# A softmax over 32768 columns: 64 KB per partition in each transfer and three buffers, in place of 32 KB and six

## The chip, the cores and the metric

The kernel runs on one core of a Trainium2 chip. Two of its engines do the arithmetic here: DVE (the vector engine) and ACT (the scalar engine). SP only issues transfers, and 16 DMA engines carry them out. The metric is device time in microseconds (us) of one execution. "Span" is the same execution as the profile sees it; it is about 1.8 us shorter than the device time.

## The reference

```python
def reference(logits, temperature):          # logits (16, 256, 32768) float32, temperature 1.0
    scaled = logits / temperature
    scaled = scaled - scaled.max(axis=-1, keepdims=True)
    exp_scaled = np.exp(scaled)
    return (exp_scaled / exp_scaled.sum(axis=-1, keepdims=True)).astype(np.float32)
```

There are 4096 rows of 128 KB each. All of them must be read once and written once: 536.87 MB in each direction, 1073.74 MB in all.

## The kernel before

A row is cut into four quarters, and 128 quarter rows (32 KB per partition, 4 MB in all) make a tile. There are 128 tiles. Neighbouring partitions hold parts of the same row, so the maximum and the sum are combined over groups of four partitions, in two rounds of shuffle and combine. Each half of a quarter has its own maximum (`nm`) and sum, and a small set of operations turns them into one factor per half (`f`).

```python
_W = 8192; _BUFS = 6; _AHEAD = 4; _CC = 4096; _SCALE_ON_DVE = {1, 4, 7}
...
        for c in range(NCH):                                  # two pieces of 4096 columns
            nc.vector.tensor_reduce(out=nm[:, c:c+1], in_=xc, axis=X, op=A.max, negate=True)
            ...
            nc.scalar.activation(out=xc, in_=xc, func=Exp, bias=nm[:, c:c+1], ..., accum_out=ssum[:, c:c+1])
        ...                                                   # 12 small DVE records more for the combines
        for c in range(NCH):
            if (t * NCH + c) % 8 in _SCALE_ON_DVE:
                nc.vector.tensor_scalar_mul(out=xc, in0=xc, scalar1=f[:, c:c+1])
            else:
                nc.scalar.activation(out=xc, in_=xc, func=Copy, scale=f[:, c:c+1])

    for t in range(min(_AHEAD, n_tiles)):
        load(t)
    for t in range(n_tiles):
        compute(t)
        store(t)
        if t + _AHEAD < n_tiles:
            load(t + _AHEAD)
```

All loads and stores are issued from one queue (SP), in program order: a load that waits for its buffer also holds up the stores that come after it.

Of the kernel before, what the change touches and what calls it, by code (L numbers as in the profile page):

```python
# [1 line left out]

# [4 lines left out]


_W = 8192
_BUFS = 6  # L10
_AHEAD = 4
_CC = 4096
_SCALE_ON_DVE = {1, 4, 7}


@with_exitstack
def kernel(
    ctx: ExitStack,
    tc: tile.TileContext,
    logits: bass.AP,  # L20
    temperature: bass.AP,
    out: bass.AP,
):
    nc = tc.nc
    inv_t = 1.0 / float(temperature)
    P = nc.NUM_PARTITIONS
    fp32 = mybir.dt.float32
    Exp = mybir.ActivationFunctionType.Exp
    Copy = mybir.ActivationFunctionType.Copy
    X = mybir.AxisListType.X  # L30
    A = mybir.AluOpType

    xf = logits.flatten_outer_dims()
    of = out.flatten_outer_dims()
    N, V = xf.shape
    W = min(_W, V)
    SPLIT = V // W
    assert SPLIT * W == V and (N * SPLIT) % P == 0 and W % _CC == 0
    x = xf.rearrange("n (h v) -> (n h) v", h=SPLIT)
    o = of.rearrange("n (h v) -> (n h) v", h=SPLIT)  # L40
    n_tiles = N * SPLIT // P
    n_rounds = SPLIT.bit_length() - 1
    NCH = W // _CC

    xpool = ctx.enter_context(tc.tile_pool(name="x", bufs=_BUFS))
    spool = ctx.enter_context(tc.tile_pool(name="stats", bufs=8))
    slots = {}

    def load(t: int) -> None:
        xs = xpool.tile([P, W], fp32, tag="x", name="xs")  # L50
        slots[t] = xs
        tc.keep_in_program_order(
            nc.sync.dma_start(out=xs, in_=x[t * P : (t + 1) * P, :])
        )

    def store(t: int) -> None:
        tc.keep_in_program_order(
            nc.sync.dma_start(out=o[t * P : (t + 1) * P, :], in_=slots.pop(t))  # L58
        )

    def combine(v, op) -> None:
        for j in range(n_rounds):
            mask = [i ^ (1 << j) for i in range(32)]
            nc.vector.stream_shuffle(  # L64
                out=v[:, j + 1 : j + 2], in_=v[:, j : j + 1], mask=mask
            )
            nc.vector.tensor_tensor(  # L67
                out=v[:, j + 1 : j + 2],
                in0=v[:, j : j + 1],
                in1=v[:, j + 1 : j + 2],  # L70
                op=op,
            )

    def compute(t: int) -> None:
        xs = slots[t]
        nm = spool.tile([P, NCH], fp32, tag="nm", name="nm")
        ssum = spool.tile([P, NCH], fp32, tag="ssum", name="ssum")
        ee = spool.tile([P, NCH], fp32, tag="ee", name="ee")
        f = spool.tile([P, NCH], fp32, tag="f", name="f")
        ttj = spool.tile([P, NCH], fp32, tag="ttj", name="ttj")  # L80
        nMh = spool.tile([P, 1 + n_rounds], fp32, tag="nMh", name="nMh")
        Sh = spool.tile([P, 1 + n_rounds], fp32, tag="Sh", name="Sh")
        rS = spool.tile([P, 1], fp32, tag="rS", name="rS")

        for c in range(NCH):
            xc = xs[:, c * _CC : (c + 1) * _CC]
            nc.vector.tensor_reduce(  # L87
                out=nm[:, c : c + 1], in_=xc, axis=X, op=A.max, negate=True
            )
            if inv_t != 1.0:  # L90
                nc.vector.tensor_scalar_mul(
                    out=nm[:, c : c + 1], in0=nm[:, c : c + 1], scalar1=inv_t
                )
            nc.scalar.activation(  # L94
                out=xc,
                in_=xc,
                func=Exp,
                bias=nm[:, c : c + 1],
                scale=inv_t,
                accum_out=ssum[:, c : c + 1],  # L100
            )

        with tc.high_priority():
            nc.vector.tensor_reduce(out=nMh[:, 0:1], in_=nm, axis=X, op=A.min)  # L104
            combine(nMh, A.min)
            nc.scalar.activation(  # L106
                out=ee,
                in_=nm,
                func=Exp,
                bias=nMh[:, n_rounds : n_rounds + 1],  # L110
                scale=-1.0,
            )
            nc.vector.tensor_tensor_reduce(  # L113
                out=ttj,
                in0=ee,
                in1=ssum,
                scale=1.0,
                scalar=0.0,
                op0=A.mult,
                op1=A.add,  # L120
                accum_out=Sh[:, 0:1],
            )
            combine(Sh, A.add)
            nc.vector.reciprocal(out=rS, in_=Sh[:, n_rounds : n_rounds + 1])  # L124
            nc.scalar.activation(out=f, in_=ee, func=Copy, scale=rS)  # L125

        for c in range(NCH):
            xc = xs[:, c * _CC : (c + 1) * _CC]
            if (t * NCH + c) % 8 in _SCALE_ON_DVE:
                nc.vector.tensor_scalar_mul(out=xc, in0=xc, scalar1=f[:, c : c + 1])  # L130
            else:
                nc.scalar.activation(out=xc, in_=xc, func=Copy, scale=f[:, c : c + 1])  # L132

    for t in range(min(_AHEAD, n_tiles)):
        load(t)
    for t in range(n_tiles):
        compute(t)
        store(t)
        if t + _AHEAD < n_tiles:
            load(t + _AHEAD)  # L140


# [1 line left out]
_INS = ['logits', 'temperature']  # L144
_OUTS = [((16, 256, 32768), 'float32')]

_NUMBERS = {'temperature': 1.0}


# [26 lines left out]
```

## Time and profile before

| | before |
|---|---|
| device time, median of the runs at hand when predicting | 2506.95 us (2502.8 to 2507.95) |
| span of the profiled run | 2500.8 us |
| DVE busy, ACT busy | 63%, 65% |
| DMA, GB/s over the span | 429 |

These are lines of the page of the kernel before: busy time and number of instruction records by engine, then the busy tenths of the DMA engines in 40 slices of the span with the GB/s that they moved, then the packets and the queues (q1 carries the kernel's own transfers, q14 the instructions).

```profile
span 2500.8 us, 4102 instructions
...
DVE 1564.4 (63%) x2400; ACT 1625.0 (65%) x929; POOL 0.2 (0%) x4
...
DMA  9999999999999999999999999999999999999997
GB/s 406 429 432 431 431 434 433 431 434 434 431 436 433 431 435 433 432 434 432 432 436 431 432 435 433 432 435 433 431 435 433 431 435 433 431 435 433 431 434 325
...
q1 hardware_dynamic: 36864, 1073.76, 99.6%
q14 instruction: 32, 0.26, 0.0%
```

DMA is at its limit from the first slice to the last, while both compute engines idle for a third of the time. The Trainium skill, "DMA: Bandwidth & Descriptors", section "Where 436 GB/s comes from", gives a ceiling of 435.2 GB/s; the trace agrees as far as it goes, no window of 600 us being above 435. The same section names about 358 GB/s on the DRAM side as what binds such transfers; this kernel moved 429 over its span, so that figure did not bind here. An estimate from the ceiling: at 435.2 GB/s the bytes need 2467 us, so a change of this kind can win at most some 34 us of the 2500.8.

The windows view splits the span into stretches. The columns are: start and end, length, busy us and instructions of DVE, ACT and POOL, PE clock, DMA share, GB/s.

```profile
400.00:1000.00 600.00, 376.43 (x582) 394.36 (x225) 0.00 (x0) 1.00 1.00 433
1000.00:1600.00 600.00, 377.06 (x581) 391.82 (x225) 0.00 (x0) 1.00 1.00 433
1600.00:2200.00 600.00, 379.09 (x573) 388.73 (x221) 0.00 (x0) 1.00 1.00 433
...
2485.00:2490.00 5.00, 0.00 (x0) 0.00 (x0) 0.00 (x0) 1.00 0.78 334
2490.00:2495.00 5.00, 0.00 (x0) 0.00 (x0) 0.00 (x0) 1.00 0.06 26
2495.00:2501.00 6.00, 0.00 (x0) 0.00 (x0) 0.00 (x0) 1.00 0.04 16
```

A share of 0.06 is one of 16 engines: one DMA engine is still working at its full 26 GB/s when the other 15 are done. A transfer is complete only when all 16 engines have done their part, so the engine that is furthest behind sets the pace of the whole kernel.

### The profile page before, as it was taken

The page shows a single profiled execution, that of the slowest core. Times are in us where ns is not written, and L with a number is a line of the kernel's source. Part 1 is how long each engine was busy: PE and PEld are TensorE (multiplying, and loading weights), DVE is VectorE, ACT ScalarE, POOL GpSimd, SP SyncE. Part 2 cuts the span into 40 slices and gives each one's busy share as a digit, 9 for nine tenths or more (in the row PEclk, how much of TensorE's full clock was granted, in tenths as well). Part 3 has the DMA queues.
Part 4 walks back from the last instruction along what each step waited for, and adds up shares of the span by engine and source line. Part 5 has one row for each costly group of instructions (what it writes and reads, how often), then busy time and mean ns, then how long its engine had stood idle before and what let it go on. Part 6 is the DMA issues. An engine that isn't in the chain of part 4 may idle for free.

```text
span 2500.8 us, 4102 instructions
## 1 busy us (share of the span) xinstructions
DVE 1564.4 (63%) x2400; ACT 1625.0 (65%) x929; POOL 0.2 (0%) x4
## 2 busy tenths in 40 slices
DVE  6666566666566665666666666666666666666564
ACT  6766666666666666666666666666666666666664
POOL 0000000000000000000000000000000000000000
DMA  9999999999999999999999999999999999999997
GB/s 406 429 432 431 431 434 433 431 434 434 431 436 433 431 435 433 432 434 432 432 436 431 432 435 433 432 435 433 431 435 433 431 435 433 431 435 433 431 434 325
DMA packets 36896, 1074.02 MB, mean 429 GB/s; under 512 B 4096, under 2 KB 4096, under 8 KB 4096
## 3 DMA queue, kind: packets, MB, share of 16 engines
q1 hardware_dynamic: 36864, 1073.76, 99.6%
q14 instruction: 32, 0.26, 0.0%
HBM read 536.87 MB, written 536.87 MB: 429 GB/s over the span
## 4 chain that ended last, share of the span: by engine, by line
DMA 76%; DVE 10%; ACT 8%; another core or an unknown queue 4%; issue 0%; SPq 0%; ACTq 0%
DMA xs<-in_logits_dram 47%; DMA out_dram<-xs 29%; DVE nm L87 9%; ACT xs L132 4%; ACT xs L94 4%; DVE Sh L67 0%; DVE Sh L64 0%; ACT f L125 0%; ACT ee L106 0%; DVE rS L124 0%; DVE ttj L113 0%; SPq L58 0%; DVE xs L130 0%; DVE nMh L67 0%
## 5 line engine op out<-in xcount | busy, mean ns | idle before, releaser
L87 DVE TENSOR_REDUCE nm<-xs 128x1 f32<-128x4096 f32 x256 | 1119.6, 4414 | 432.9 <-DMA xs<-in_logits_dram 432.9
L94 ACT ACTIVATE xs<-xs,nm 128x4096 f32<-128x4096 f32 x256 | 949.1, 3707 | 677.5 <-DVE nm L87 677.5
L132 ACT ACTIVATE xs<-xs,f 128x4096 f32<-128x4096 f32 x160 | 589.9, 3705 | 4.1
L113 DVE CUSTOM_DVE_ANT_0 ttj<-ee,ssum 128x2 f32<-128x2 f32 x128 | 20.5, 160 | 391.5 <-ACT ee L106 382.9
L130 DVE TENSOR_SCALAR xs<-xs,f 128x4096 f32<-128x4096 f32 x96 | 225.9, 2353 | 41.0 <-ACT f L125 39.7
L125 ACT ACTIVATE f<-ee,rS 128x2 f32<-128x2 f32 x128 | 37.8, 295 | 159.0 <-DVE rS L124 159.0
L94 ACT ACTIVATION_READ_ACCUMULATOR xs<-xs,nm 128x1 f32 x256 | 47.7, 187 | 0.0
L67 DVE TENSOR_TENSOR nMh<-nMh 128x1 f32<-128x1 f32 x256 | 40.8, 159 | 8.6
L67 DVE TENSOR_TENSOR Sh<-Sh 128x1 f32<-128x1 f32 x256 | 40.8, 159 | 8.6
L64 DVE STREAM_SHUFFLE nMh<-nMh 128x1 f32<-128x1 f32 x256 | 38.8, 151 | 0.0
L64 DVE STREAM_SHUFFLE Sh<-Sh 128x1 f32<-128x1 f32 x256 | 38.7, 151 | 0.0
L106 ACT ACTIVATE ee<-nm,nMh 128x2 f32<-128x2 f32 x128 | 35.8, 280 | 0.0
L124 DVE RECIPROCAL rS<-Sh 128x1 f32<-128x1 f32 x128 | 21.0, 164 | 4.3
L104 DVE TENSOR_REDUCE nMh<-nm 128x1 f32<-128x2 f32 x128 | 19.8, 155 | 4.3
L113 DVE DVE_READ_ACCUMULATOR2_ANT Sh<- 128x1 f32 x128 | 10.6, 83 | 0.0
L64 DVE LOAD_MASK_SELECT Sh<-Sh x256 | 3.6, 14 | 10.8
L64 DVE LOAD_MASK_SELECT nMh<-nMh x256 | 3.6, 14 | 10.8
L94 ACT ACT_TABLE_LOAD x1 | 1.3, 1283 | 13.1 <-DMA xs<-in_logits_dram 13.1
L157 POOL MEMSET const-bfloat16-1.0<- 128x1 bf16 x1 | 0.1, 101 | 0.0
L157 POOL MEMSET const-uint8-127<- 128x1 uint8 x1 | 0.1, 101 | 0.0
L157 POOL MEMSET const-float32-0.0<- 128x1 f32 x1 | 0.1, 98 | 0.2 <-issue 0.2
L157 POOL MEMSET const-float32-1.0<- 128x1 f32 x1 | 0.1, 98 | 0.0
## 6 DMA issues: line engine op xcount, KB each, us to landing
xs<-in_logits_dram SPq DMA_DIRECT2D x128, 4096.0 KB, 48.4
out_dram<-xs SPq DMA_DIRECT2D x128, 4096.0 KB, 49.6
```

Of the source, the lines that this page charges most:

```text
L64: nc.vector.stream_shuffle(out=v[:, j + 1 : j + 2], in_=v[:, j : j + 1], mask=mask)
L67: nc.vector.tensor_tensor(out=v[:, j + 1 : j + 2], in0=v[:, j : j + 1], in1=v[:, j + 1 : j + 2], op=op,)
L87: nc.vector.tensor_reduce(out=nm[:, c : c + 1], in_=xc, axis=X, op=A.max, negate=True)
L94: nc.scalar.activation(out=xc, in_=xc, func=Exp, bias=nm[:, c : c + 1], scale=inv_t, accum_out=ssum[:, c : c + 1],)
L104: nc.vector.tensor_reduce(out=nMh[:, 0:1], in_=nm, axis=X, op=A.min)
L106: nc.scalar.activation(out=ee, in_=nm, func=Exp, bias=nMh[:, n_rounds : n_rounds + 1], scale=-1.0,)
L113: nc.vector.tensor_tensor_reduce(out=ttj, in0=ee, in1=ssum, scale=1.0, scalar=0.0, op0=A.mult, op1=A.add, accum_out=Sh[:, 0:1],)
L124: nc.vector.reciprocal(out=rS, in_=Sh[:, n_rounds : n_rounds + 1])
L125: nc.scalar.activation(out=f, in_=ee, func=Copy, scale=rS)
L130: nc.vector.tensor_scalar_mul(out=xc, in0=xc, scalar1=f[:, c : c + 1])
L132: nc.scalar.activation(out=xc, in_=xc, func=Copy, scale=f[:, c : c + 1])
L157: nc = _bacc.Bacc("TRN2", target_bir_lowering=False, num_devices=1)
```

## The change

The intent is fewer and larger packets, half as many small operations, and a shorter start and end. A tile becomes 128 half rows (64 KB per partition, 8 MB), of which three fit. The loads of the first and last tiles and the last store are moved in pieces of 16 KB per partition. A tile has four pieces of 4096 columns, each scaled by DVE (2560 columns) and ACT (1536 columns) together. The multiplication that makes the factors moves from ACT to DVE. Only one round of combining is left.

```diff
-_W = 8192
-_BUFS = 6
-_AHEAD = 4
-_CC = 4096
-_SCALE_ON_DVE = {1, 4, 7}
+_SPLIT = 2
+_CW = 16384
+_BUFS = 3
+_PIECE = 4096
+_LAST_DMA = 4096
+_DVE_SHARE = 0.625
 ...
+    def load(i: int) -> None:
+        g, c = divmod(i, C)
+        xs = xpool.tile([P, CW], fp32, tag="x", name="xs")
+        slots[i] = xs
+        for s, n in spans(CW, _LAST_DMA if g in (0, G - 1) else CW):
+            ... nc.sync.dma_start(out=xs[:, s : s + n], in_=x[...])
 ...
-            nc.scalar.activation(out=f, in_=ee, func=Copy, scale=rS)
+            nc.vector.tensor_scalar_mul(out=f, in0=ee, scalar1=rS)
 ...
+            cut = int(n * _DVE_SHARE) // 512 * 512
+            nc.vector.tensor_scalar_mul(
+                out=xs[:, s : s + cut], in0=xs[:, s : s + cut], scalar1=f[:, k : k + 1]
+            )
+            nc.scalar.activation(
+                out=xs[:, s + cut : s + n], in_=xs[:, s + cut : s + n],
+                func=Copy, scale=f[:, k : k + 1],
+            )
 ...
+    order = [("L", i) for i in range(min(_BUFS, n_chunks))] + [("S", 0)]
+    for i in range(1, n_chunks):
+        order.append(("S", i))
+        if i + _BUFS - 1 < n_chunks:
+            order.append(("L", i + _BUFS - 1))
```

More of the change, by code (lines that the diff above doesn't have):

```diff
@@ L35, with spans, piece, store @@
     N, V = xf.shape
-    W = min(_W, V)
-    SPLIT = V // W
-    assert SPLIT * W == V and (N * SPLIT) % P == 0 and W % _CC == 0
-    x = xf.rearrange("n (h v) -> (n h) v", h=SPLIT)
-    o = of.rearrange("n (h v) -> (n h) v", h=SPLIT)
-    n_tiles = N * SPLIT // P
-    n_rounds = SPLIT.bit_length() - 1
-    NCH = W // _CC
+    W = V // _SPLIT
+    CW = min(_CW, W)
+    C = W // CW
+    assert W * _SPLIT == V and CW * C == W and (N * _SPLIT) % P == 0
+    x = xf.rearrange("n (h v) -> (n h) v", h=_SPLIT)
+    o = of.rearrange("n (h v) -> (n h) v", h=_SPLIT)
+    G = N * _SPLIT // P
+    n_chunks = G * C
+    n_rounds = _SPLIT.bit_length() - 1
     xpool = ctx.enter_context(tc.tile_pool(name="x", bufs=_BUFS))
-    spool = ctx.enter_context(tc.tile_pool(name="stats", bufs=8))
+    spool = ctx.enter_context(tc.tile_pool(name="stats", bufs=3))
     slots = {}
-    def load(t: int) -> None:
-        xs = xpool.tile([P, W], fp32, tag="x", name="xs")
-        slots[t] = xs
-        tc.keep_in_program_order(
-            nc.sync.dma_start(out=xs, in_=x[t * P : (t + 1) * P, :])
-        )
-    def store(t: int) -> None:
-        tc.keep_in_program_order(
-            nc.sync.dma_start(out=o[t * P : (t + 1) * P, :], in_=slots.pop(t))
-        )
+    stats = {}
+    def spans(total: int, step: int) -> list[tuple[int, int]]:
+        return [(s, min(step, total - s)) for s in range(0, total, step)]
+    def piece(g: int) -> int:
+        return _PIECE if g < G - 1 else min(_PIECE, _LAST_DMA)
+    def load(i: int) -> None:
[3 more added lines that the diff above has]
+        for s, n in spans(CW, _LAST_DMA if g in (0, G - 1) else CW):
+            tc.keep_in_program_order(
+                nc.sync.dma_start(
+                    out=xs[:, s : s + n],
+                    in_=x[g * P : (g + 1) * P, c * CW + s : c * CW + s + n],
+                )
+            )
+    def store(i: int) -> None:
+        g, c = divmod(i, C)
+        xs = slots.pop(i)
+        for s, n in spans(CW, _LAST_DMA if g == G - 1 else CW):
+            tc.keep_in_program_order(
+                nc.sync.dma_start(
+                    out=o[g * P : (g + 1) * P, c * CW + s : c * CW + s + n],
+                    in_=xs[:, s : s + n],
+                )
+            )
     def combine(v, op) -> None:
@@ L72, in combine, with exps, factors @@
             )
-    def compute(t: int) -> None:
-        xs = slots[t]
-        nm = spool.tile([P, NCH], fp32, tag="nm", name="nm")
-        ssum = spool.tile([P, NCH], fp32, tag="ssum", name="ssum")
-        ee = spool.tile([P, NCH], fp32, tag="ee", name="ee")
-        f = spool.tile([P, NCH], fp32, tag="f", name="f")
-        ttj = spool.tile([P, NCH], fp32, tag="ttj", name="ttj")
+    def exps(i: int) -> None:
+        g, c = divmod(i, C)
+        xs = slots[i]
+        ps = spans(CW, piece(g))
+        K = C * len(ps)
+        if c == 0:
+            stats[g] = tuple(
+                spool.tile([P, K], fp32, tag=f"{nm}{K}", name=nm)
+                for nm in ("nm", "ssum", "ee", "f", "ttj")
+            )
+        nm, ssum = stats[g][:2]
+        for j, (s, n) in enumerate(ps):
+            k = c * len(ps) + j
+            nc.vector.tensor_reduce(
+                out=nm[:, k : k + 1], in_=xs[:, s : s + n], axis=X, op=A.max, negate=True
+            )
+            if inv_t != 1.0:
+                nc.vector.tensor_scalar_mul(
+                    out=nm[:, k : k + 1], in0=nm[:, k : k + 1], scalar1=inv_t
+                )
+            nc.scalar.activation(
+                out=xs[:, s : s + n],
+                in_=xs[:, s : s + n],
+                func=Exp,
+                bias=nm[:, k : k + 1],
+                scale=inv_t,
+                accum_out=ssum[:, k : k + 1],
+            )
+    def factors(g: int) -> None:
+        nm, ssum, ee, f, ttj = stats[g]
         nMh = spool.tile([P, 1 + n_rounds], fp32, tag="nMh", name="nMh")
@@ L83, in compute @@
         rS = spool.tile([P, 1], fp32, tag="rS", name="rS")
-        for c in range(NCH):
-            xc = xs[:, c * _CC : (c + 1) * _CC]
-            nc.vector.tensor_reduce(
-                out=nm[:, c : c + 1], in_=xc, axis=X, op=A.max, negate=True
-            )
-            if inv_t != 1.0:
-                nc.vector.tensor_scalar_mul(
-                    out=nm[:, c : c + 1], in0=nm[:, c : c + 1], scalar1=inv_t
-                )
-            nc.scalar.activation(
-                out=xc,
-                in_=xc,
-                func=Exp,
-                bias=nm[:, c : c + 1],
-                scale=inv_t,
-                accum_out=ssum[:, c : c + 1],
-            )
         with tc.high_priority():
@@ L124, in compute, with scales @@
             nc.vector.reciprocal(out=rS, in_=Sh[:, n_rounds : n_rounds + 1])
-            nc.scalar.activation(out=f, in_=ee, func=Copy, scale=rS)
-        for c in range(NCH):
-            xc = xs[:, c * _CC : (c + 1) * _CC]
-            if (t * NCH + c) % 8 in _SCALE_ON_DVE:
-                nc.vector.tensor_scalar_mul(out=xc, in0=xc, scalar1=f[:, c : c + 1])
-            else:
-                nc.scalar.activation(out=xc, in_=xc, func=Copy, scale=f[:, c : c + 1])
-    for t in range(min(_AHEAD, n_tiles)):
-        load(t)
-    for t in range(n_tiles):
-        compute(t)
-        store(t)
-        if t + _AHEAD < n_tiles:
-            load(t + _AHEAD)
+            nc.vector.tensor_scalar_mul(out=f, in0=ee, scalar1=rS)
+    def scales(i: int) -> None:
+        g, c = divmod(i, C)
+        xs = slots[i]
+        f = stats[g][3]
+        ps = spans(CW, piece(g))
+        for j, (s, n) in enumerate(ps):
+            k = c * len(ps) + j
+            cut = int(n * _DVE_SHARE) // 512 * 512
+            nc.vector.tensor_scalar_mul(
+                out=xs[:, s : s + cut], in0=xs[:, s : s + cut], scalar1=f[:, k : k + 1]
+            )
+            nc.scalar.activation(
+                out=xs[:, s + cut : s + n],
+                in_=xs[:, s + cut : s + n],
+                func=Copy,
+                scale=f[:, k : k + 1],
+            )
+    order = [("L", i) for i in range(min(_BUFS, n_chunks))] + [("S", 0)]
[3 more added lines that the diff above has]
+            order.append(("L", i + _BUFS - 1))
+    nxt = 0
+    done = -1
+    loaded = 0
+    for kind, i in order:
+        if kind == "L":
+            load(i)
+            loaded = i + 1
+        else:
+            g = i // C
+            if g > done:
+                while nxt < (g + 1) * C:
+                    assert nxt < loaded
+                    exps(nxt)
+                    nxt += 1
+                factors(g)
+                done = g
+            scales(i)
+            store(i)
 _INS = ['logits', 'temperature']
```

## The prediction

> **What bounds the kernel now.** The DMA engines. The page's slices show DMA at 9 tenths throughout; the windows view gives 433 GB/s in every long stretch, while DVE is busy 63% and ACT 65%. The kernel moves 1073.7 MB. The Trainium skill, "DMA: Bandwidth & Descriptors", section "Where 436 GB/s comes from", puts the ceiling at 435.2 GB/s; that would be 2467 us, so 34 of the 2500.8 us of span can be had (no long window of the trace is above 433).
>
> Where the 34 us are (packet records and semaphore landings of the trace):
> - A 32 KB packet follows the last one after 1209.4 ns; 32768 B at 27.2 GB/s are 1204.7. An 8 KB packet took 309 ns, a 32 KB one 1213; together they give about 4 ns per packet besides the bytes. Each DMA engine has 2048 packets: 8 to 10 us. The skill's section "Why small descriptors are slow" describes such a fixed cost, some 3 cycles per packet.
> - One DMA engine falls behind. The last of a transfer's 16 landings is 0.1 us after the second last at the start, 9 us at the end, and from 2490 to 2500 us the windows view shows a DMA share of 0.06, one engine of 16. From 688 us on the slowest landing slips by about 0.95 us 14 times, some 125 us apart, each shortly after an 8 KB packet of the instruction queue. DVE has 2400 instruction records, so about 19 such fetches: 18 us on that engine. I take these to be DVE's instructions, all on one engine. Sum for it: 2048 x 1.2094 + 18 + 2.3 (completions of 9 ns) + start 2.2 = 2499.5; its last data packet ends at 2499.6.
>
> **What the change does.**
> - 64 KB per packet: half the per-packet cost, estimate -4.3 us; nothing if a row goes as two packets.
> - DVE records per 8 MB go from about 38 to 19 (one set of small operations instead of two, one shuffle round instead of two). 1216 records, about 10 fetches: -8.5 us on the slow engine. This I expect to be the main gain.
> - Fewer completions (about 140 instead of 256): -1 us.
> - Latency of a tile grows: 4 maxima 17.7 us, last exponential 3.9, factors about 2, scaling about 6 (DVE 2560 columns: 1.47 us from 2.35 for 4096; ACT 1536 columns about 1.5): 30 us from landing to store. In queue order the store of tile i must be there 38.6 us after load i landed (a store and a load of 8 MB lie between): about 6 us are spare, three buffers suffice.
> - Ends: the first piece lands near 8 us instead of 13, worth nothing, as loads fill the queue until 60 us. At the end the last tile's compute hides behind the store of the tile before it.
>
> On the critical path are only the slow DMA engine's packets. Engine work stays hidden; DVE goes to about 64%, ACT to about 57%.
>
> **Prediction.** 2506 - 14 = 2492 us, range 2480 to 2505. Faster by over 2%: 0.01; within 2%: 0.96; slower by over 2%: 0.03.
>
> **What would show it.** 64 KB packets (about 20,000 in all) of 2.41 us; 434 GB/s in the middle; half as many instruction packets; lag of the last engine about 5 us instead of 9; no wait of the store issues that leaves DMA below 9 tenths.
>
> **What would make it wrong.** Bubbles because the tile latency passes 38 us; 64 KB rows split or slower per byte; another engine lagging for reasons of its own.

## The result, and the profile after

| | before | after |
|---|---|---|
| device time, median of 4 runs | 2505.12 us | 2504.49 us (2502.32 to 2508.87) |
| span of the profiled run | 2500.8 us | 2504.7 us |
| DVE records | 2400 | 1216 |

The ratio of the times is 0.9999, with a 95% interval of 0.9979 to 1.0019. Here and below, a ratio is the mean time of one kernel's fast runs over that of the other's of the same rounds, so it is not quite the ratio of the medians. A gain of 14 us was forecast, and there is none. The profile of the kernel before fell on a fast run (2502.6 us), that of the changed kernel on a slower one (2506.49 us): the two profiles differ by 3.9 us where the times do not.

These are the same lines of the page of the changed kernel:

```profile
span 2504.7 us, 2498 instructions
...
DVE 1579.7 (63%) x1216; ACT 1368.7 (55%) x833; POOL 0.2 (0%) x4
...
DMA  9999999999999999999999999999999999999998
GB/s 419 434 426 433 429 436 434 436 434 433 435 434 434 429 428 433 433 434 422 433 422 431 434 423 432 433 422 434 429 425 434 423 433 432 423 433 432 423 422 375
...
q1 hardware_dynamic: 19728, 1073.75, 99.8%
q14 instruction: 20, 0.16, 0.0%
```

The packets and the instruction fetches fell as intended. But the row of GB/s has holes of 422 to 426 in its second half, at a DMA share that still reads 9. The windows view of the same kernel puts a number on it:

```profile
400.00:1000.00 600.00, 383.26 (x292) 334.49 (x202) 0.00 (x0) 1.00 1.00 433
1000.00:1600.00 600.00, 377.04 (x296) 327.51 (x202) 0.00 (x0) 1.00 1.00 430
1600.00:2200.00 600.00, 378.70 (x287) 324.30 (x197) 0.00 (x0) 1.00 1.00 430
...
2500.00:2505.00 5.00, 0.00 (x0) 0.00 (x0) 0.00 (x0) 1.00 0.06 26
```

The engines count as busy, yet they move 430 GB/s instead of 433: some packets take longer. To see which, one has to go below the views, to the records of single packets and of the semaphore increments. Each transfer ends with 16 increments, one per DMA engine. From those records, summed by direction and place in the transfer, this is what I computed:

```
                               before   after
usual time of a packet, ns       1213    2418    (32 KB and 64 KB)
stretch per DMA engine, us        4.7    20.6    (all time above the usual, summed, over 16)
lateness of the last engine, us  14.4    25.6    (70 to 2400 us: its landings against
                                                  packets back to back, 9.684 us
                                                  for 4 MB, 19.322 us for 8 MB)
```

In the changed kernel 17.5 of the 20.6 us sit in the eighth and last packet of a transfer, just before the direction changes from load to store or back. Of the 25.6 us of lateness, 24.5 lie at ends of loads. Nine landings among them are late by 0.96 to 0.98 us each, 8.7 us together, and follow an instruction fetch by 11 to 13 us. The other 15.8 us are steps of up to 0.94 us at the ends of loads. The prediction has no term for those.

The timeline shows how closely a store comes before it is needed. First the kernel before: a store is issued at 1195.96 us, and the section on DMA issues says how long such a store takes from issue to landing (the last column, median us).

```profile
1195.96 0.34 SPq L58 DMA_DIRECT2D out_dram<-xs  x1
```

```profile
out_dram<-xs SPq DMA_DIRECT2D x128, 4096.0 KB, 49.6
```

A store of 4 MB needs 9.7 us of that, so it stands in the queue for about 40 us. Now the timeline of the changed kernel, one tile: the maxima start when the load has landed, the store follows, and the next load lands at 1018.79 us.

```profile
979.61 17.40 DVE L107 TENSOR_REDUCE nm<-xs 128x1 f32<-128x4096 f32 x4 [10.36 <-DMA xs<-in_logits_dram]
...
1002.13 5.94 DVE L160 TENSOR_SCALAR xs<-xs,f 128x2560 f32<-128x2560 f32 x4
...
1008.18 0.33 SPq L75 DMA_DIRECT2D out_dram<-xs  x1
1008.56 0.43 SPq L64 DMA_DIRECT2D xs<-in_logits_dram  x1
1018.79 17.40 DVE L107 TENSOR_REDUCE nm<-xs 128x1 f32<-128x4096 f32 x4 [10.72 <-DMA xs<-in_logits_dram]
```

The store is issued 28.6 us after its tile has landed, as predicted, and 10.6 us before the last engine has finished the load that precedes it. I call this the margin; over all tiles its median is 10.4 us. No engine runs dry for more than a fraction of a microsecond, and that rarely. For the engines in front, though, the store is only just there: 13 of the 16 landings of that load come at 1010.0 to 1010.6 us, and three follow 5 to 9 us later. It is at those three that the last packet of the load is stretched.

Two theories were left, and a third came later. LATE: stores that come so late stretch the last packets, although nobody waits. PACKET: 64 KB packets are stretched as such. TRAFFIC: the compute engines' own use of the on-chip memory stretches them. Beside them stood the theory that carried most of the forecast gain, FETCH: each fetch of DVE instructions costs one DMA engine about 0.95 us.

### The profile page after: what moved, and what is told of

The parts are those of the page before. It is cut to its first block, busy times and chain, and to the rows that moved or that the text cites. A ratio compares the mean times of both kernels' runs of the same rounds, so it can differ in the third digit from the quotient of the medians.

```text
span 2504.7 us, 2498 instructions
## 1 busy us (share of the span) xinstructions
DVE 1579.7 (63%) x1216; ACT 1368.7 (55%) x833; POOL 0.2 (0%) x4
## 2 busy tenths in 40 slices
DMA packets 19748, 1073.91 MB, mean 429 GB/s; under 512 B 2192, under 2 KB 2192, under 8 KB 2192
## 4 chain that ended last, share of the span: by engine, by line
DMA 74%; DVE 14%; ACT 10%; SPq 1%; issue 0%; ACTq 0%; another core or an unknown queue 0%
DMA xs<-in_logits_dram 72%; DVE nm L107 13%; ACT xs L163 7%; ACT xs L114 3%; DMA out_dram<-xs 2%; SPq L75 1%; DVE xs L160 0%; DVE f L150 0%; ACT ee L131 0%; DVE rS L149 0%; DVE Sh L87 0%; DVE Sh L84 0%; DVE ttj L138 0%; ACTq L224 0%
## 5 line engine op out<-in xcount | busy, mean ns | idle before, releaser
L163 ACT ACTIVATE xs<-xs,f 128x1536 f32<-128x1536 f32 x256 | 382.3, 1564 | 73.5 <-DVE f L150 73.5
L160 DVE TENSOR_SCALAR xs<-xs,f 128x2560 f32<-128x2560 f32 x256 | 380.2, 1549 | 2.6 <-DVE f L150 0.4
L138 DVE CUSTOM_DVE_ANT_0 ttj<-ee,ssum 128x4 f32<-128x4 f32 x64 | 10.4, 162 | 222.4 <-ACT ee L131 222.4
L131 ACT ACTIVATE ee<-nm,nMh 128x4 f32<-128x4 f32 x64 | 18.0, 282 | 0.0
L150 DVE TENSOR_SCALAR f<-ee,rS 128x4 f32<-128x4 f32 x64 | 14.7, 229 | 2.2
L149 DVE RECIPROCAL rS<-Sh 128x1 f32<-128x1 f32 x64 | 10.5, 164 | 2.2
L87 DVE TENSOR_TENSOR Sh<-Sh 128x1 f32<-128x1 f32 x64 | 10.2, 160 | 2.2
L87 DVE TENSOR_TENSOR nMh<-nMh 128x1 f32<-128x1 f32 x64 | 10.2, 160 | 2.2
L129 DVE TENSOR_REDUCE nMh<-nm 128x1 f32<-128x4 f32 x64 | 10.1, 157 | 2.2
L84 DVE STREAM_SHUFFLE nMh<-nMh 128x1 f32<-128x1 f32 x64 | 9.7, 151 | 0.0
L84 DVE STREAM_SHUFFLE Sh<-Sh 128x1 f32<-128x1 f32 x64 | 9.7, 151 | 0.0
```

The source lines that it names most:

```text
L84: nc.vector.stream_shuffle(out=v[:, j + 1 : j + 2], in_=v[:, j : j + 1], mask=mask)
L87: nc.vector.tensor_tensor(out=v[:, j + 1 : j + 2], in0=v[:, j : j + 1], in1=v[:, j + 1 : j + 2], op=op,)
L129: nc.vector.tensor_reduce(out=nMh[:, 0:1], in_=nm, axis=X, op=A.min)
L131: nc.scalar.activation(out=ee, in_=nm, func=Exp, bias=nMh[:, n_rounds : n_rounds + 1], scale=-1.0,)
L138: nc.vector.tensor_tensor_reduce(out=ttj, in0=ee, in1=ssum, scale=1.0, scalar=0.0, op0=A.mult, op1=A.add, accum_out=Sh[:, 0:1],)
L149: nc.vector.reciprocal(out=rS, in_=Sh[:, n_rounds : n_rounds + 1])
```

## The experiments

"Before" in a comparison is always the kernel before, run on the same chip in the same rounds.

### a_narrow: the same instructions on fewer columns

```diff
-                out=nm[:, k : k + 1], in_=xs[:, s : s + n], axis=X, op=A.max, negate=True
+                out=nm[:, k : k + 1], in_=xs[:, s : s + n // 8], axis=X, op=A.max, negate=True
     (and the exponentials and scales likewise: an eighth of the columns)
```

> The changed kernel with the same instructions, transfers and buffers, but each large operation works on an eighth of its columns (wrong result on purpose), so a store is issued some 20 us earlier after its load. Theory LATE (stores come so late with three buffers that the DMA engines meet the end of a load with hardly anything queued, and the last packets of a transfer are stretched): the stretched packets go, span 2485 to 2490 us, about 15 us below the kernel before. Rival PACKET (the stretch comes with 64 KB packets as such): 2500 to 2507 us as the changed kernel, last packets still stretched.

Measured: 2492.76 us median, ratio 0.9950 (0.9935 to 0.9965), span 2491.1 us (1 us above the range expected by LATE), result wrong. The timeline shows the store at 984.88 us, and the load before it lands at 1017.06 us: a margin of 32 us.

```profile
984.88 0.33 SPq L75 DMA_DIRECT2D out_dram<-xs  x1
...
1017.06 2.46 DVE L107 TENSOR_REDUCE nm<-xs 128x1 f32<-128x512 f32 x4 [32.48 <-DMA xs<-in_logits_dram]
```

The windows of the same run are back at full rate:

```profile
1000.00:1600.00 600.00, 77.10 (x287) 69.25 (x196) 0.00 (x0) 1.00 1.00 434
1600.00:2200.00 600.00, 80.45 (x303) 73.56 (x208) 0.00 (x0) 1.00 1.00 434
```

The stretch per engine fell from 20.6 to 4.7 us and the lateness of the last engine from 25.6 to 12.0 us. So the 64 KB packets, the three buffers and the order are all able to give 2493 us. This is what the prediction said, without the prediction's reason for believing it. PACKET falls as a sufficient cause. But this kernel also took away memory traffic, so TRAFFIC was not excluded.

### b_32k_late and c_32k_early: two transfers of 32 KB per tile

```diff
-        for s, n in spans(CW, _LAST_DMA if g in (0, G - 1) else CW):
+        for s, n in (spans(CW, _LAST_DMA) if g in (0, G - 1) else spans(CW, 8192)):
     (stores likewise; in b_32k_late the spans of both are reversed)
```

> The changed kernel with each transfer of 64 KB per partition sent as two of 32 KB, second half first for loads and stores, so that computing still starts only when the whole tile is there. LATE: no gain, 2500 to 2510 us (32 KB packets cost 5 us more in themselves). PACKET: stretched packets go, 2488 to 2493 us.

> As b_32k_late, but first half first: the maxima of the first half can start 9.7 us before the tile is complete, so the stores come about 9 us earlier. LATE: most of the stretch goes, 2490 to 2496 us, and clearly faster than b_32k_late. PACKET: same as b_32k_late.

Measured: b 2497.59 us, ratio 0.9971 (0.9956 to 0.9985); c 2498.20 us, ratio 0.9972 (0.9955 to 0.9988). Both were correct. The stretch per engine was 5.4 and 5.5 us. At first sight this speaks for PACKET, as the two are alike. But the trace of b shows that it is not late: its first maxima start 9.7 us before the tile is complete, because the scheduler took the pieces in the order in which they land. The margins were 18.8 us in b and 21.7 us in c. So b missed its aim. It is a second early kernel, not a late one, and says nothing about PACKET. The time of b lies in neither of its two ranges, that of c 2 us above the range that LATE gave it. The pair shows that with all of the compute in place the stretch can go. As it has both smaller packets and 8 to 11 us more of margin than the changed kernel, it cannot by itself say which of the two did it.

### d_before_pad: a test of FETCH that tested something else

```diff
         compute(t)
+        for _ in range(19):
+            nc.vector.tensor_scalar_mul(out=pad[:, 0:1], in0=pad[:, 1:2], scalar1=1.0)
         store(t)
```

> The kernel before with 19 tiny DVE instructions more per tile (2432 in all, one column each, DVE has time for them), which doubles DVE's instruction records. Theory FETCH (each fetch of 8 KB of DVE instructions costs the same one DMA engine about 0.95 us, and that engine sets the end): about 19 fetches more, plus 15 to 19 us, 2520 to 2524 us, the last engine's lag grows from 9 to some 25 us. Rival (fetches are hidden, the lag has another cause): 2503 to 2508 us.

Measured: 2683.49 us, ratio 1.0713. This is far beyond either theory. The slices of the page say why: in the first third of the span DVE is at 8 to 9 tenths and DMA falls as low as 6.

```profile
DVE  9899898998977766566666656666666656666663
...
DMA  8997776867789999999999999999999999999998
```

The padding depended on nothing, so the scheduler moved it forward: all of it ran in the first 746 us. DVE became the limit there. The run is no test of FETCH.

### e_nocombine and f_before_pad2: DVE's instruction count, down and up

```diff
 e_nocombine:
-            combine(nMh, A.min)
 ...
-            combine(Sh, A.add)
 f_before_pad2 (at the end of compute):
+        for _ in range(19):
+            nc.vector.tensor_scalar_mul(out=pad, in0=f[:, 0:1], scalar1=1.0)
```

> The kernel before without the two combines over partitions (wrong result on purpose): 12 DVE instruction records fewer in each of 128 tiles, 864 instead of 2400, transfers and buffers unchanged. FETCH (each fetch of DVE instructions costs one DMA engine 0.95 us, and that engine ends last): 12 fetches fewer, 10 to 12 us less, 2492 to 2496 us, lag of the last engine a few us. Rival (fetches don't set the end): 2503 to 2508 us, lag unchanged.

> The padding repeated so that it cannot bunch up: 19 tiny DVE instructions after each tile's own factors (2432 in all), 3 us of DVE time per tile of 19.4 us, of which DVE needed 12. The first padded kernel is no test, as its padding piled up in the first 850 us and left DMA idle. FETCH: 19 fetches more, 15 to 19 us more, 2520 to 2525 us, DMA at 9 tenths throughout. Rival: 2503 to 2510 us.

Measured: e_nocombine 2494.36 us, ratio 0.9955 (0.9940 to 0.9969), result wrong; f_before_pad2 2517.49 us, ratio 1.0046 (1.0031 to 1.0061), correct. The queue lines of the two pages give the fetches, 12 fewer and 19 more than the 32 of before. First e_nocombine:

```profile
DVE 1407.0 (56%) x864; ACT 1624.9 (65%) x929; POOL 0.2 (0%) x4
...
q14 instruction: 20, 0.16, 0.0%
```

Then f_before_pad2:

```profile
DVE 1918.1 (76%) x4832; ACT 1625.2 (65%) x929; POOL 0.2 (0%) x4
...
q14 instruction: 51, 0.42, 0.0%
```

In f_before_pad2 DMA stayed at 9 tenths in all slices but the last, and the windows view reads 433 GB/s in every long stretch, so nothing else was in the way. The ratios are worth 11 us less and 12 us more on 2506 us: 0.94 us per fetch removed and 0.6 us per fetch added. The second is smaller than expected. In the profiled runs alone they are (2500.8 - 2492.4) / 12 = 0.7 us and (2515.8 - 2500.8) / 19 = 0.8 us. FETCH stands in direction on both sides; the size, 0.6 to 0.94 us, is known less well than the 0.95 us assumed. The lag shows it too: the time between the ninth and the last of a transfer's 16 landings, at 95% of the run, is 13.0 us in the kernel before, 7.1 in e_nocombine and 29.7 in f_before_pad2. One correction to the prediction: not DVE's records alone set the number of fetches. The pages count 4102, 2568, 6535 and (changed kernel) 2498 instructions of all engines; divided by 128 that is 32.0, 20.1, 51.1 and 19.5, against 32, 20, 51 and 20 fetches. DVE has most of them, so its count moved the most.

### g_half: half the dose

```diff
     as a_narrow, with n // 2 in place of n // 8
```

> A dose between the changed kernel and a_narrow: large operations on half of their columns (wrong result on purpose), so stores come some 13 us earlier than in the changed kernel, 64 KB packets and buffers unchanged. LATE: stretch per engine near that of a_narrow (5 us), 2491 to 2496 us. If only the extreme case helps: 2498 to 2505 us.

Measured: 2493.70 us, ratio 0.9953 (0.9937 to 0.9970), stretch per engine 4.1 us, margin 22.8 us, result wrong. Half of the narrowing has all of its effect. With 64 KB packets both ways the damage sets in somewhere between margins of 22.8 and 10.4 us.

### h_six32: six buffers of 32 KB

```diff
-_CW = 16384
-_BUFS = 3
+_CW = 8192
+_BUFS = 6
```

> The changed kernel with six buffers of 32 KB per partition in place of three of 64 KB, half a row being two of them (correct result): 32 KB packets, half the DVE records of the kernel before, a load can follow the store of half a tile. Candidate for the best of all. LATE and PACKET both: like c_32k_early or a little better, 2490 to 2497 us. If a change of direction of the transfers itself costs (load, store, load, store in 32 KB steps, twice as many changes): worse than c_32k_early, 2500 us or more.

Measured: 2528.36 us, ratio 1.0087 (1.0065 to 1.0108), correct. The stretch per engine is 30.7 us, more than in the changed kernel, with 32 KB packets. So 64 KB packets aren't needed for the stretch, and PACKET is down a second time. But the stores aren't late here: the margin is 29 us. What is late is something else. The queue's own waits:

```profile
SPq L64 <- DMA out_dram<-xs: 2296.7, 122, 33.1
SPq L75 <- DVE xs L160: 75.1, 8, 30.7
```

The issuing queue stands nearly all the time before a load whose buffer is still being stored, and the store that comes after this load in program order leaves the moment the load may go:

```profile
1806.69 0.34 SPq L64 DMA_DIRECT2D xs<-in_logits_dram  x1
1807.13 0.40 SPq L75 DMA_DIRECT2D out_dram<-xs  x1
```

LATE as I put it, with stores alone, does not cover this kernel. Two other causes can be checked against traces. Changes of direction, the rival of the expectation, were to give 2500 us or more, and did. But the kernel before alternates single loads and stores of 32 KB packets just as often, with a stretch of 4.7 us, so this alone is not enough. Nor is it the pairing: in c_32k_early the next load is also issued 0.4 us after the store, and the stretch is 5.5 us. What h_six32 shares with the other stretched kernels is that its loads come late. Call the time from a load's issue to the last landing of the store before it the load margin: it is 19.4 us here, 29.3 in the changed kernel, and 36 to 40 us in every kernel with a stretch of 4 to 6 us (the table below).

### k_32k_whole: 32 KB packets and late stores, this time truly late

```diff
+    def view(g, xs, s, n):       # a piece takes columns of both halves of the tile
+        if g == G - 1:
+            return xs[:, s : s + n]
+        return xs.rearrange("p (h v) -> p h v", h=2)[:, :, s // 2 : (s + n) // 2]
     (used by the maxima, exponentials and scales; transfers as in c_32k_early)
```

> b_32k_late did not do what it was made for: its trace shows the first maximum 9.7 us before the tile is complete, as in c_32k_early, because the scheduler took the pieces in the order in which they land. Here every piece takes columns of both halves, so that nothing can start before the whole tile is there: 32 KB packets and 30 us from landing to store as in the changed kernel. LATE: the stretch is back, loads of the last engine some 15 us late in sum, 2505 to 2512 us (32 KB packets cost 5 us more). PACKET: as b_32k_late and c_32k_early, 2495 to 2499 us.

Measured: 2507.75 us median, with single runs at 2499.58, 2505.96, 2509.54 and 2518.73; ratio 1.0025 (1.0001 to 1.0049), correct. The margin is 10.1 us. The mean lies about 10 us above that of c_32k_early, which has the same packets, the same work and a margin of 21.7 us. This is what LATE expects. The spread is wider than that of any other kernel, and the profile fell on the fastest of the four (stretch 9.3 us per engine). So the stretch in the slow runs of this kernel was not seen. (The two kernels ran on different chips, each against the kernel before.)

### n_narrow_delay: the time put back without the traffic

```diff
     a_narrow, and before the factors of each tile:
+            for a, b in ((0, 16384), (0, 6144)):
+                nc.vector.tensor_reduce(
+                    out=rS[0:1, 0:1], in_=slots[g][0:1, a:b], axis=X, op=A.max
+                )
```

> a_narrow (2491 to 2493 us) with the time put back but not the traffic: two maxima over one partition only, 16384 and 6144 columns, some 24 us of DVE per tile, keep the stores as late as in the changed kernel (wrong result on purpose). LATE (late stores alone stretch the last packets of loads): 2499 to 2507 us, loads of the last engine 10 us or more late in sum. Rival TRAFFIC (the SBUF traffic of the full computing stretches them): 2491 to 2494 us.

Measured: 2509.52 us median (2503.80 to 2509.89), ratio 1.0011 (0.9996 to 1.0026), result wrong. The timeline shows the delay, the store and the landing of the load before it:

```profile
984.76 17.21 DVE L130 TENSOR_REDUCE rS<-xs 1x1 f32<-1x16384 f32 x1 [0.64 <-ACT xs L114]
1002.00 6.54 DVE L130 TENSOR_REDUCE rS<-xs 1x1 f32<-1x6144 f32 x1
...
1010.89 0.33 SPq L75 DMA_DIRECT2D out_dram<-xs  x1
...
1020.76 2.46 DVE L107 TENSOR_REDUCE nm<-xs 128x1 f32<-128x512 f32 x4 [10.18 <-DMA xs<-in_logits_dram]
```

The windows fall below the changed kernel's:

```profile
1000.00:1600.00 600.00, 439.69 (x328) 70.59 (x199) 0.00 (x0) 1.00 1.00 430
1600.00:2200.00 600.00, 434.12 (x324) 72.22 (x204) 0.00 (x0) 1.00 1.00 428
```

This is the experiment that settles the cause as far as it is settled. Against a_narrow, only time was added, on one partition of 128, and 17 us came back (by the medians; 15 by the ratios; about 1 us of it can be the one fetch more that the added records bring, 21 against 20). The delay makes the load late as well as the store, since the load follows the store in the queue: the load margin fell from 38.6 to 28.1 us. The pattern came back as well. The next table is computed from the packet records: the mean stretch of the last packet of a load, by how long before that packet's end the next store was issued.

```
store issued ... us before    0-2    2-4    4-6    6-8    8-10   20-26  28-30
changed kernel, ns              0     46    101    181     252
n_narrow_delay, ns              0     28    149    310     306
a_narrow, ns                                                     0 to 2    74
```

The table leaves out the packets of a_narrow that end 30 to 34 us after the issue; they are stretched by some 140 ns. So compare at the same place: packets that end 4 to 7 us behind the first landing of their load (100 to 2400 us) are stretched by 0.33 us in the changed kernel, 0.42 in n_narrow_delay and 0.04 in a_narrow. The engines in front meet the store within 2 us of its issue and pay nothing at the end of the load; in both late kernels it is their last packet of the store that is stretched, by 0.3 to 0.4 us. That this costs nothing, as they are in front, is argued and not tested. The engines behind, which set the time, pay 0.1 to 0.3 us at the end of nearly every load. TRAFFIC falls: it is not needed for the stretch here, and m_best below has all of it with a stretch of 4.6 us.

### m_best and m2_best: a version that beats both

```diff
 m_best: loads of the middle tiles in two halves, stores whole
-        for s, n in spans(CW, _LAST_DMA if g in (0, G - 1) else CW):
+        for s, n in spans(CW, _LAST_DMA if g in (0, G - 1) else 8192):
 m2_best: also
-            nc.vector.tensor_scalar_mul(out=f, in0=ee, scalar1=rS)
+            nc.scalar.activation(out=f, in_=ee, func=Copy, scale=rS)
     and whole pieces scaled in turn by ACT and DVE, in place of each piece by both
```

> Candidate for the best: the changed kernel with loads in two halves of 32 KB (computing starts early, stores come 9 us earlier) and stores in one piece of 64 KB. By LATE: like c_32k_early less 2.4 us of packet cost, 2493 to 2497 us.

> As m_best, with whole pieces scaled in turn by DVE and ACT and the factors multiplied on ACT: 16 DVE records per tile instead of 19, about 1.5 fetches fewer. FETCH: 1 to 2 us less than m_best, within what can be told apart, if the stores, which come about 1 us later, cost nothing.

Measured over 5 runs each: m_best 2496.10 us, ratio 0.9964 (0.9951 to 0.9976); m2_best 2495.32 us, ratio 0.9961 (0.9948 to 0.9973). Both were correct and had margins of 18.8 and 17.4 us and a stretch of 4.6 and 4.7 us per engine. They beat the kernel before by 9 to 10 us; the changed kernel, which no run told from the kernel before, was not in these rounds. The two can't be told apart from each other.

### p_early_delay: a dose too large

```diff
     c_32k_early, and before the factors of each tile:
+                nc.vector.tensor_reduce(out=rS[0:1, 0:1], in_=slots[g][0:1, 0:8192], axis=X, op=A.max)
```

> c_32k_early (2497 to 2498.5 us) with one maximum over one partition and 8192 columns, 8.8 us of DVE per tile, before the factors, so that stores come about 8 us later, with 32 KB packets and all traffic unchanged. LATE: slower by several us and more scattered, mean 2502 to 2510 us, like k_32k_whole. TRAFFIC or PACKET: 2497 to 2500 us.

Measured: 2627.99 us, ratio 1.0490, correct. The delay had to wait for the first exponentials in DVE's order, and 3.9 us of waiting came with its 8.7. A tile then took longer than the queue's 38.7 us for a store and a load. Its stores follow each other by 40.9 us in the timeline, and the packet records show the engines truly idle for about 1.2 us before each store, where the changed kernel has only rare gaps, nearly all under 0.5 us. The stretch per engine is 56.7 us. It does not tell LATE from the others. It does show the cliff that the prediction feared, and that the changed kernel is on the near side of it.

### q_after_again: the changed kernel a second time

> The changed kernel once more: 2500 to 2509 us as before, and a second profile of the stretch, 10 to 20 us per engine; if its span is near 2500 us, the loads of the last engine should be late by less than the 24.5 us of the first profile, by about as much as the span is shorter.

Measured: 2507.60 us median (2503.20 to 2509.30), ratio 1.0006 (0.9991 to 1.0021). The second profile has a span of 2507.5 us, a stretch per engine of 23.5 us (expected were 10 to 20) and a lateness of the last engine of 28.3 us, of which nine steps behind fetches make 8.7. Both profiles of the changed kernel agree. The span was not near 2500 us, so the condition of that expectation did not arise.

The profiled runs whose engines do not run dry, in one table (the changed kernel's second profile, q_after_again, in brackets; k_32k_whole is the fastest of its four runs):

```
                  margin of  margin of  stretch per   lateness of the        span
                  store, us  load, us   engine, us    last engine, us        us
before            39.9       38.7        4.7          14.4                   2500.8
changed           10.4       29.3       20.6 (23.5)   25.6  (28.3)           2504.7  (2507.5)
a_narrow          32.1       38.6        4.7          12.0                   2491.1
g_half            22.8       38.6        4.1          11.7                   2490.7
n_narrow_delay     9.2       28.1       23.9          28.0                   2507.6
b_32k_late        18.8       37.2        5.4          10.6                   2495.0
c_32k_early       21.7       37.7        5.5          11.9                   2496.7
k_32k_whole       10.1       28.6        9.3          12.3                   2497.8
h_six32           29.2       19.4       30.7          42.1                   2530.3
m_best            18.8       37.7        4.6          12.4                   2494.3
m2_best           17.4       36.3        4.7          10.6                   2493.0
e_nocombine       40.7       38.7        4.1           6.0                   2492.4
f_before_pad2     38.4       39.5        5.4          28.9                   2515.8
```

The margin of the load sorts all rows: 36 us and more go with a stretch of 4 to 6 us, 28 to 30 us with 9 to 24, 19 us with 31. The margin of the store does not sort h_six32. In every other stretched kernel both margins are short, so no run tells whether a late store alone would stretch packets. f_before_pad2 shows the other road to a late last engine: fetches, without stretch.

## Why the prediction was right or wrong

- **DMA sets the time, and the last engine sets DMA's.** Right. Among kernels of the table with the same packet size, the spans follow the lateness of the engine that is furthest behind.
- **64 KB per packet, -4.3 us.** Right. Packets of 64 KB follow each other after 2414 ns, two of 32 KB after 2 x 1209.4 = 2418.8 ns; times 1024 packets that is 5 us. There were 19748 packets in all, so a row is one packet.
- **Half the DVE records, -8.5 us.** Right in direction and number: nine landings of the last engine slip by 0.97 us each in the changed kernel, where I had put ten fetches. The gain itself was not measured alone; at the 0.6 to 0.94 us per fetch of e_nocombine and f_before_pad2, nine fetches fewer are worth 5 to 8.5 us. The Trainium skill, "CRC Debugging", section "Comparing the Two Runs", calls the transfers of queue 14 instruction refills; that their number is the instruction count over 128 in four kernels (32, 20, 20 and 51) agrees with this.
- **Latency of a tile.** The estimate of 30 us was right (28.6), and so was the conclusion that the queue does not run dry.
- **"About 6 us are spare, three buffers suffice."** This is the step that failed. It assumed that a store costs nothing as long as it is issued before the engines need it. The spare time was larger than I thought (10.4 us) and did not suffice. With stores, and the loads issued behind them, that late, the last packets of loads are stretched at the engines behind: steps of 15.8 us at the last engine from 70 to 2400 us. This took back the gains forecast for packets, fetches and completions (4.3 + 8.5 + 1 us). n_narrow_delay against a_narrow shows that lateness is enough by itself: 15 to 17 us for 24 us of delay, with traffic, packets and nearly all instructions alike. Whether the late store or the late load does it stays open.
- **What would show it.** "434 GB/s in the middle" was the line that failed: 433, then 430. "No wait of the store issues that leaves DMA below 9 tenths" held, and was the wrong thing to watch, as stretched packets count as busy. The lag of the last engine behind the second last was forecast at 5 us instead of 9; it was 2.2 at the end, as others fell behind too. Instruction packets were forecast at half and were 20 of 32, since the other engines' instructions stayed.
- **"DVE goes to about 64%, ACT to about 57%."** Measured were 63% and 55%.
- **Class and range.** "Within 2%" was right, and 2504.49 us lies just inside the range of 2480 to 2505. The forecast of a gain of 14 us was wrong.

Open are: what in a DMA engine stretches the last packet before a change of direction when the next transfer was issued late; whether the late store or the late load behind it does the harm (h_six32, with early stores, speaks for the load); and why k_32k_whole scatters over 19 us. I have no experiment for the first that kernels alone could make.

## What to carry to other kernels

In a kernel that is bound by DMA, the time of a transfer's issue matters before anything waits for it: in this kernel's order of one store and one load of 8 MB, 10 us of margin for the store (29 for the load) cost about 15 us over the run, and 17 to 23 us (36 and more for the load) cost nearly nothing. So begin the work on a tile when its first half has landed, rather than add packet size, and look at the loads as well: h_six32 had 29 us of margin for its stores, 19 for its loads, and lost 22 us. Read such a kernel by the GB/s of its long windows and by the DMA engine that ends last, not by the busy share. And count instructions: here every 128 records are one fetch, and a fetch of DVE's cost one DMA engine 0.6 to 0.97 us, which counts once that engine is the last.

## What the Trainium skill lacked or had wrong

- "DMA: Bandwidth & Descriptors" says that small transfers should be made one large one and that a DMA should be issued early (section "Rules for kernel authors"), but not how early, nor that lateness costs before an engine runs dry. Here, with 64 KB per partition, a margin of 9 us for the store and 28 for the load cost 15 to 17 us in 2500 (n_narrow_delay 2509.52 us against a_narrow 2492.76); 23 and 39 us cost nothing that could be seen (g_half).
- The same page, section "Queues, rings and completion order", names instruction refill among the users of queue row 14, but no page gives its price to the kernel's own transfers: 0.6 to 0.94 us per fetch of 8 KB on one DMA engine (e_nocombine, 12 fetches fewer, ratio 0.9955; f_before_pad2, 19 more, ratio 1.0046), with one fetch per 128 instructions (4102, 2498, 2568 and 6535 instructions: 32, 20, 20 and 51 fetches).
- No page that I found says how far the 16 DMA engines of a transfer drift apart within one kernel: the last of 16 landings came 0.1 us after the second last at the start of the kernel before, and 8.6 us after it, 13.0 us after the ninth, at 95%.
